# One core, two blocks: attention scores of block 1 and chunk updates of the gated linear attention as fp32r products of stacked parts

## The chip, the cores and the metric

The kernel runs on one core of one Trainium2 chip. The metric is the device time of one execution in microseconds, the median of several runs. Five engines work from queues of their own: TensorE (PE; its weight loads are listed as PEld), VectorE (DVE), ScalarE (ACT), GpSimd (POOL) and SyncE (SP, which here issues the DMAs).

## The reference, cut to what matters

The program computes two transformer blocks in fp32 on 512 tokens of width 1024. The first has 16 meta tokens ahead of the sequence and mixes by sliding-window attention (16 query heads of 64, 4 key heads, sinks) beside a state-space layer; the second has a latent attention and a gated linear attention. The two places that matter:

```python
def block_fn(args):
    n, qn, kn, vn = args
    keys = jnp.concatenate([k_meta, kn], axis=1)
    vals = jnp.concatenate([v_meta, vn], axis=1)
    sc = jnp.einsum('bqkgd,bskd->bkgqs', qn, keys).astype(jnp.float32)
    ...
    p = sink_softmax(sc, mask, sink)
    return jnp.einsum('bkgqs,bskd->bqkgd', p.astype(vals.dtype), vals)
...
    k_dec = k * jnp.exp(tot[:, :, None] - cum).astype(k.dtype)
    upd = jnp.einsum('bnchk,bnchv->nbhkv', k_dec, v).astype(jnp.float32)
    def step(state, inp):
        g, u, qc = inp
        state = state * g[..., None] + u
        return state, jnp.einsum('bchk,bhkv->bchv', qc, state)
```

The first is the attention of 128 queries over 16 meta keys and 256 others; the second the update of the gated linear attention's state by chunks of 64 tokens.

## The kernel before, in words

**Products in three parts.** A fp32 operand is held as two fp32r tiles, a high part and the rest. `fetch` (L144) brings 512 KB of weights into `raw`, ScalarE copies the high part `whi`, VectorE subtracts for `wlo`. A product with weights is three fp32r matmuls: high by high, high by low, low by high (`mm3` L175, `proj` L185, `nat` L190). Products of two activations mostly stay fp32 and show two records each in the trace.

**Order.** The program is written as one sequence; a scheduler orders each engine's queue ahead of time, and the queues do not change at run time. `ps_b`, `ps_q`, `ps_t`, `ps_o` are PSUM banks: in the attention 2, 3, 2 and 1 of them (L679).

**Attention of block 1 (L648 to L804).** Keys: `proj` gives 128 rows, two key heads of 64; each is copied into a tile `kw` of its own whose other 64 rows are zero (L651 to L678), by POOL for one head and ScalarE for the other, in three windows of 16 meta keys and 256 keys. Values are taken by `nat` (L686). `query` (L700) projects 128 rows, two heads of 64 that belong to different key heads, and scales them on VectorE into `q`. There are 8 queries: four ahead and four among the units. A unit is a pair of key heads and 128 tokens, 8 units in all. `scores1` (L716) makes 8 products of 128x272 (128x144 in a first unit of a pair), `q` against `kw` in fp32 (L727), and VectorE adds the mask and takes the maximum (L730). Then the sink, the exponentials on ScalarE and the scaling follow, separately for the two key heads, with ten operations of four columns on VectorE. `turn1` transposes (L759, L769), the results leave PSUM on VectorE for one head and on ScalarE for the other (L771, L773), and `values1` multiplies by the values (L781, L785). The state-space layer (`ssm_quarter`, L569 to L600) is worked in four quarters between the units: its products L569 go through `ps_b`, VectorE takes them out into `sq`, and L591, L592 use what it makes of them.

**Gated linear attention (L1300 to L1420).** `values` (L1344) takes value tokens, 24 matmuls of 256 columns to a group of 128 tokens, and ScalarE copies the group to `gv`; `keys` (L1348) multiplies the decay `ek` by the keys in place on VectorE. `recur` (L1362) forms for each of 4 heads, 4 blocks and 2 chunks the update `ek` x `gv` in fp32 on 64 rows of the array (L1370; the two chunks of a block use the two halves of the rows), VectorE adds it to the state (L1379), and L1381 multiplies by the queries. Value, key, gate and query groups of other heads fill the time between.

Of the kernel before, what the change touches and what calls it, by code (L numbers as in the profile page):

```python
# [9 lines left out]
F32 = mybir.dt.float32  # L10
# [8 lines left out]
P = 128  # L19
D = 1024  # L20
KD = D // P
S = 512
# [31 lines left out]
def body(nc, tc, A, out, es):  # L54
# [593 lines left out]
    with tc.tile_pool(name="m1", bufs=1) as mp:  # L648
        att = mp.tile([P, 8, S], F32, name="att")
        with tc.tile_pool(name="m2", bufs=1) as ap_:  # L650
            kz = [[ap_.tile([P, 3, 272], F32, name=f"kw{mo}{e}") for e in range(2)] for mo in range(2)]  # L651
            for gs in kz:
                for e, g in enumerate(gs):
                    GP.memset(g[64 - 64 * e:128 - 64 * e], 0.0)
# [9 lines left out]
            kw = []  # L664
            for mo in range(2):
                p = proj(wload("w_in", 1024), P, 0, z, C528)
                f = ap_.tile([P, T1], F32, name="kf", tag=f"sq{mo}")
                mul(v2(f), p[:, :, :264], v2(R))

                gs = kz[mo]  # L670
                for e, g in enumerate(gs):
                    r_ = slice(64 * e, 64 * e + 64)
                    cpy = (lambda o, i: act(o, i, AF.Copy)) if e else GP.tensor_copy
                    cpy(g[r_, 0], f[r_, :272])
                    GP.tensor_copy(g[r_, 1:, 0:NM], f[r_, 0:NM].unsqueeze(1).to_broadcast([64, 2, NM]))
                    for n in range(1, 3):
                        cpy(g[r_, n, NM:], f[r_, NM + n * P:NM + (n + 2) * P])
                kw.append(gs)  # L678
# [19 lines left out]
            qf = []  # L698

            def query():  # L700
                p = proj(wload("w_in", 1024), P, 0, z, C512)
                t = (mp if len(qf) < 2 else ap_).tile([P, S], F32, name=f"q{len(qf)}")
                stt(t, p[:, 0, :], 0.125, Rr, ALU.mult, ALU.mult)
                qf.append(t)

            for _ in range(4):
                query()
# [8 lines left out]
            def scores1(u):  # L716
# [861 lines left out]
```

## Time and profile before

| | us |
|---|---|
| median of 3 runs (2582.31 to 2583.71) | 2582.53 |
| the profiled execution's own time | 2580.72 |
| its span | 2578.9 |
| PE busy | 2558.5 (99%) |
| DVE busy | 1577.0 (61%) |
| ACT busy | 993.6 (39%) |
| POOL busy | 84.8 (3%) |

The granted clock of PE was 0.999 of full speed over the span. The span is what the trace covers; the execution's own time lies 1.8 us above it. A matmul's duration is longer than the distance from its start to the next one's, because matmuls overlap in the array; what a matmul costs is therefore read from starts.

### The profile page before, as it was taken

Reading aid. Unit: us, or ns where it says so; the run is one execution under the profiler, and the core shown is the slowest. Engines: PE = TensorE matmul, PEld = TensorE weight load, DVE = VectorE, ACT = ScalarE, POOL = GpSimd, SP = SyncE. Lnnn points to the kernel's source line nnn. Section 1 sums busy time; section 2 is a strip of 40 time slices with the busy share of each in tenths; the row PEclk is TensorE's granted clock in tenths of the full one; section 3 lists DMA queues with packets and bytes.
Section 4 is the critical chain, followed back from the end, with each engine's and each line's share of the span. In section 5 each row is a group of like instructions: output and inputs, shape, how many; then the busy total and the mean of one; then the engine's idle time right before and its main releaser. Section 6 shows DMA issues by size and latency. Waiting matters only on the chain.

```text
span 2578.9 us, 34903 instructions
## 1 busy us (share of the span) xinstructions
PE 2558.5 (99%) x13914; PEld 2181.4 (85%) x13914; DVE 1577.0 (61%) x2866; ACT 993.6 (39%) x1560; POOL 84.8 (3%) x98
## 2 busy tenths in 40 slices
PE   9999999999999999999999999999999999999999
PEld 9999999766888888888888888888878888888887
DVE  7985445685457544468665775555763457655566
ACT  5222223445333222236554454333353234433333
POOL 0000001000000000000000001000000010100000
PEclk9999999999999999999999999999999999999999
DMA  5443324332333333332112223333232222333332
GB/s 183 132 135 110 97 91 135 105 97 63 105 98 96 97 98 98 98 94 70 54 58 62 75 81 108 97 98 98 82 101 66 74 60 83 120 98 98 98 92 73
DMA packets 80774, 243.64 MB, mean 94 GB/s; under 512 B 10418, under 2 KB 20530, under 8 KB 80483
## 3 DMA queue, kind: packets, MB, share of 16 engines
q1 hardware_dynamic: 80610, 241.40, 30.8%
q8 instruction: 110, 1.80, 0.3%
q14 instruction: 54, 0.43, 0.1%
HBM read 229.44 MB, written 11.93 MB: 94 GB/s over the span
## 4 chain that ended last, share of the span: by engine, by line
PE 97%; DVE 2%; ACT 0%; issue 0%; DMA 0%; SPq 0%; DVEq 0%; ACTq 0%
PE ps_b L182 27%; PE ps_q L182 19%; PE ps_t L182 18%; PE mm L182 16%; PE ps_b L198 5%; PE ps_o L1240 1%; PE ps_q L1212 1%; PE ps_q L727 1%; PE ps_o L785 1%; PE ps_t L1228 1%; PE ps_q L1370 1%; DVE sq L66 1%; DVE h L66 0%; PE ps_t L769 0%; PE ps_b L1443 0%; PE ps_q L198 0%
## 5 line engine op out<-in xcount | busy, mean ns | idle before, releaser
L86 ACT ACTIVATE whi<-raw 128x1024 fp32r<-128x1024 f32 (+2 forms) x418 | 432.6, 1038 | 980.9 <-PE ps_b L182 276.3
L66 DVE TENSOR_TENSOR wlo<-raw,whi 128x1024 fp32r<-128x1024 f32 (+2 forms) x418 | 502.4, 1204 | 328.8 <-ACT whi L86 326.6
L182 PE MATMUL ps_b<-zh,whi 128*128 128x512 f32 (+1 forms) x692 | 272.9, 394 | 2.3 <-ACT att L86 0.7
L182 PE MATMUL ps_b<-zl,whi 128*128 128x512 f32 (+1 forms) x692 | 269.7, 390 | 0.0
L182 PE MATMUL ps_b<-zh,wlo 128*128 128x512 f32 (+1 forms) x692 | 269.1, 389 | 0.0
L182 PE MATMUL ps_q<-zh,whi 128*128 128x512 f32 (+1 forms) x488 | 189.3, 388 | 1.2 <-ACT zh L86 1.2
L182 PE MATMUL ps_q<-zl,whi 128*128 128x512 f32 (+1 forms) x488 | 189.4, 388 | 0.0
L182 PE MATMUL ps_q<-zh,wlo 128*128 128x512 f32 (+1 forms) x488 | 189.2, 388 | 0.0
L182 PE MATMUL ps_t<-zh,whi 128*128 128x512 f32 x476 | 185.6, 390 | 0.6 <-ACT zh L86 0.6
L182 PE MATMUL ps_t<-zl,whi 128*128 128x512 f32 x476 | 185.5, 390 | 0.0
L182 PE MATMUL ps_t<-zh,wlo 128*128 128x512 f32 x476 | 185.2, 389 | 0.0
L182 PE MATMUL mm<-zh,whi 128*128 128x264 f32 x800 | 162.5, 284 | 5.7 <-ACT whi L86 5.7
L182 PE MATMUL mm<-zl,whi 128*128 128x264 f32 x800 | 161.8, 284 | 0.0
L182 PE MATMUL mm<-zh,wlo 128*128 128x264 f32 x800 | 161.2, 283 | 0.0
L182 PEld LDWEIGHTS ps_b<-zh,whi 128*128 128x128 f32 (+1 forms) x692 | 129.2, 187 | 33.8 <-issue 2.5
L182 PEld LDWEIGHTS ps_b<-zh,wlo 128*128 128x128 f32 (+1 forms) x692 | 129.2, 187 | 28.6 <-issue 1.1
L182 PEld LDWEIGHTS ps_b<-zl,whi 128*128 128x128 f32 (+1 forms) x692 | 129.3, 187 | 27.2 <-issue 0.7
L182 PEld LDWEIGHTS mm<-zh,whi 128*128 128x128 f32 x800 | 124.3, 189 | 5.8 <-ACT whi L86 5.7
L182 PEld LDWEIGHTS mm<-zl,whi 128*128 128x128 f32 x800 | 124.1, 189 | 0.3 <-DVE zl L83 0.3
L182 PEld LDWEIGHTS mm<-zh,wlo 128*128 128x128 f32 x800 | 124.0, 189 | 0.0
L182 PEld LDWEIGHTS ps_q<-zh,whi 128*128 128x128 f32 x488 | 91.6, 188 | 20.8 <-ACT zh L86 2.0
L182 PEld LDWEIGHTS ps_q<-zl,whi 128*128 128x128 f32 x488 | 91.6, 188 | 20.4 <-DVE zl L66 1.3
(581 smaller groups left out, 5322.2 us busy)
## 6 DMA issues: line engine op xcount, KB each, us to landing
raw<-in_ffn_w_dram SPq DMA_DIRECT2D x130, 512.0 KB, 3.5
raw<-in_w_up_dram SPq DMA_DIRECT2D x88, 512.0 KB, 3.6
raw<-in_w_down_dram SPq DMA_DIRECT2D x44, 512.0 KB, 3.6
raw<-in_w_in_dram SPq DMA_DIRECT2D x32, 512.0 KB, 3.5
raw<-in_mla_o_dram SPq DMA_DIRECT2D x16, 512.0 KB, 3.6
raw<-in_ple_g_dram SPq DMA_DIRECT2D x16, 512.0 KB, 3.7
raw<-in_glu_dram SPq DMA_DIRECT2D x8, 512.0 KB, 3.5
raw<-in_w_out_dram SPq DMA_DIRECT2D x8, 512.0 KB, 3.5
```

Of the source, the lines that this page charges most:

```text
L66: return (e or V).tensor_tensor(o, a, b, op=op)
L86: return SC.activation(o, a, f, **kw)
L182: last["pe"] = PE.matmul(o[:, i, :c1 - c0], lhs, x[k][r][:, c0:c1], start=(k == 0 and j == 0), stop=(k == kt - 1 and j == 2))
L198: PE.matmul(o[:m, :n], x[k][a][:, t0:t0 + m], w[b][:, kk_ * c + m0:kk_ * c + m0 + n], start=(k == 0 and i == 0), stop=(k == kt - 1 and i = ...
L727: last["sc"] = PE.matmul(pq[s_][:, :W], qf[pp * 4 + i][:, n * P:(n + 1) * P], kw[pp][s_][:, max(n - 1, 0), :W])
L785: PE.matmul(po[64 * s_:64 * s_ + 64], vb[n - 1 + j][:, kv * 64:kv * 64 + 64], pT[s_][:, j], start=False, stop=(j == 1))
L1212: PE.matmul(p[:, :N], d["q"][e][:, bs], d["k"][e][:, :N], start=False, stop=True)
L1228: PE.transpose(pt[:, kt * P:(kt + 1) * P], sc[:, kt * P:(kt + 1) * P], ident)
L1240: PE.matmul(po[:, b * P:(b + 1) * P], vt[:, kt, e * P:(e + 1) * P], pT[:, kt * P:(kt + 1) * P], start=(kt == 0), stop=(kt == b))
L1370: PE.matmul(pu[c][:, :256], ek[b][rows, hc], vt[hh][rows, b])
```

## The change

**Attention of block 1.** Both parts of a key head now lie doubled on 128 rows: `kh` holds the high part on both halves, `kl` the rest on both. A unit builds two query tiles `qs`, each of four heads, with the high part in one half of the rows and the rest in the other half. A score is then `qs` x `kh` plus `qs` x `kl`, two fp32r products of 272 columns, or of 256 in a first unit of a pair. `keys(0)` is built ahead of the values, `keys(1)` after the scores of the fourth unit, in the same buffers. The query's scaling is a ScalarE copy; the scale of the norm is applied where the maximum is taken, as a pointer, and the sink is the start of that maximum. The statistics of two heads share a tile of eight columns, with four small operations on VectorE and one small exponential to a unit. All transposed results leave PSUM on ScalarE. Four weight tiles are fetched ahead of the keys.

**Gated linear attention.** The key tile is split into `kd`, high part and rest stacked on 128 rows, one per chunk; the values become `gvh` (high part on both halves, four ScalarE copies to a group) and `gvl` (the rest on the own half, zero on the other, two VectorE subtractions). An update is two fp32r products on all 128 rows.

```diff
-        att = mp.tile([P, 8, S], F32, name="att")
+        att = [mp.tile([P, 4, S], F32, name="att0")]
         with tc.tile_pool(name="m2", bufs=1) as ap_:
-            kz = [[ap_.tile([P, 3, 272], F32, name=f"kw{mo}{e}") for e in range(2)] for mo in range(2)]
-            for gs in kz:
-                for e, g in enumerate(gs):
-                    GP.memset(g[64 - 64 * e:128 - 64 * e], 0.0)
...
+            for _ in range(4):
+                fetch("w_in", 1024)
+            kf = []
             for mo in range(2):
                 p = proj(wload("w_in", 1024), P, 0, z, C528)
-                f = ap_.tile([P, T1], F32, name="kf", tag=f"sq{mo}")
+                f = zp.tile([P, aw], F32, name="acc") if mo else ap_.tile([P, T1], F32, name="kf", tag="sq0")
                 mul(v2(f), p[:, :, :264], v2(R))
-
-                gs = kz[mo]
-                for e, g in enumerate(gs):
-                    r_ = slice(64 * e, 64 * e + 64)
-                    cpy = (lambda o, i: act(o, i, AF.Copy)) if e else GP.tensor_copy
-                    cpy(g[r_, 0], f[r_, :272])
-                    GP.tensor_copy(g[r_, 1:, 0:NM], f[r_, 0:NM].unsqueeze(1).to_broadcast([64, 2, NM]))
-                    for n in range(1, 3):
-                        cpy(g[r_, n, NM:], f[r_, NM + n * P:NM + (n + 2) * P])
-                kw.append(gs)
+                kf.append(f)
+
+            def keys(pp):
+
+                out_ = []
+                for e in range(2):
+                    a = slice(64 * e, 64 * e + 64)
+                    f = kf[pp][a]
+                    kh, kl = (ap_.tile([P, 3, 272], F32R, name=f"k{n}{e}") for n in "hl")
+                    for o in (a, slice(64 - 64 * e, 128 - 64 * e)):
+                        for w_, c in ((0, f[:, :272]), *((n, f[:, NM + n * P:NM + (n + 2) * P]) for n in (1, 2))):
+                            t = slice(NM if w_ else 0, 272)
+                            act(kh[o, w_, t], c, AF.Copy)
+                            sub(kl[o, w_, t], c, kh[a, w_, t].bitcast(F32))
+                        for k in (kh, kl):
+                            GP.tensor_copy(k[o, 1:, :NM], k[o, 0:1, :NM].to_broadcast([64, 2, NM]))
+                    out_.append((kh, kl))
+                return out_
+
+            kw = {0: keys(0)}
...
-            qf = []
-
-            def query():
+            qf = [mp.tile([P, 4, S], F32, name=f"q{i}") for i in range(2)]
+
+            def query(i):
                 p = proj(wload("w_in", 1024), P, 0, z, C512)
-                t = (mp if len(qf) < 2 else ap_).tile([P, S], F32, name=f"q{len(qf)}")
-                stt(t, p[:, 0, :], 0.125, Rr, ALU.mult, ALU.mult)
-                qf.append(t)
-
-            for _ in range(4):
-                query()
+                act(qf[i // 4][:, i % 4], p[:, 0], AF.Copy, scale=0.125)
+
+            for i in range(4):
+                query(i)
...
-                st = [[sm.tile([P, 4], F32, name=f"at{j}{s_}", bufs=2) for j in range(3)] for s_ in range(2)]
+                mx, dn, nb = (sm.tile([P, 8], F32, name=f"at{j}", bufs=2) for j in range(3))
+                sk = sink[:, pp * 8:pp * 8 + 8]
+
+                qs = []
+                for s_ in range(2):
+                    t = ap_.tile([P, 4, P], F32R, name=f"qs{s_}", bufs=2)
+                    a, o = slice(64 * s_, 64 * s_ + 64), slice(64 - 64 * s_, 128 - 64 * s_)
+                    x = qf[pp][a, :, n * P:(n + 1) * P]
+                    act(t[a], x, AF.Copy)
+                    sub(t[o], x, t[a].bitcast(F32))
+                    qs.append(t)
                 for i in range(4):
                     pq = [pss("q"), pss("q")]
                     for s_ in range(2):
-                        last["sc"] = PE.matmul(pq[s_][:, :W], qf[pp * 4 + i][:, n * P:(n + 1) * P],
-                                               kw[pp][s_][:, max(n - 1, 0), :W])
+                        for k in range(2):
+                            last["sc"] = PE.matmul(pq[s_][:, :max(W, 256)], qs[s_][:, i],
+                                                   kw[pp][s_][k][:, max(n - 1, 0), :max(W, 256)],
+                                                   start=(k == 0), stop=(k == 1))
                     for s_ in range(2):
-                        V.tensor_tensor_reduce(sc[s_][:, i, :W], pq[s_][:, :W], mk, 1.0, -3.0e38,
-                                               ALU.add, ALU.max, st[s_][0][:, i:i + 1])
+                        c = s_ * 4 + i
+                        V.tensor_tensor_reduce(sc[s_][:, i, :W], pq[s_][:, :W], mk, r[:, n:n + 1], sk[:, c:c + 1],
+                                               ALU.add, ALU.max, mx[:, c:c + 1])
+                ts(nb, mx, -1.0)
+                sub(mx, sk, mx)
+                act(mx, mx, AF.Exp)
                 for s_ in range(2):
-                    mx, dn, nb = st[s_]
...
-                    tt(mx, mx, sk, ALU.max)
-                    ts(nb, mx, -1.0)
-                    sub(mx, sk, mx)
-                    act(mx, mx, AF.Exp)
...
-                    add(dn, dn, mx)
-                    V.reciprocal(dn, dn)
...
+                add(dn, dn, mx)
+                V.reciprocal(dn, dn)
...
                 live[u] = sc, mt
...
-                        if s_:
-                            V.tensor_copy(pT[:, j], pt)
-                        else:
-                            act(pT[:, j], pt, AF.Copy)
+                        act(pT[:, j], pt, AF.Copy)
...
-                act(att[:, pp * 4:pp * 4 + 4, n * P:(n + 1) * P], po.rearrange("p (i q) -> p i q", i=4), AF.Copy)
+                act(att[pp][:, :, n * P:(n + 1) * P], po.rearrange("p (i q) -> p i q", i=4), AF.Copy)
...
-                    query()
+                    query(4 + ui)
+                if ui == 3:
+                    kw[1] = keys(1)
+                if ui == 4:
+                    att.append(mp.tile([P, 4, S], F32, name="att1", tag="q0"))
                 elif 5 <= ui < 8:
                     gate(zp.tile([P, aw], F32, name="acc" if ui == 5 else "sq", bufs=1 if ui == 5 else 2)[:, :S])
                 elif ui == 8:
+                    gt = mp.tile([P, 4, S], F32, name="gt", tag="q1")
                     with tc.issue_after(last["sc"].ins):
                         for i in range(2):
-                            gate(mp.tile([P, S], F32, name=f"q{i}"))
+                            gate(gt[:, i])
...
+        kd = [[mp.tile([P, S], F32R, name=f"kd{b}{c}", bufs=1) for c in range(2)] for b in range(4)]
+        ch = lambda c: slice(64 * c, 64 * c + 64)
+        vl = [mp.tile([P, 2, 256], F32R, name=f"gvl{i}", bufs=1) for i in range(6)]
+        for t in vl:
+            for c in range(2):
+                ts(t[ch(1 - c), c], mask[ch(1 - c), :256], 0.0)
...
-            t = qt[i] = mp.tile([P, 4, 2, P], F32, name=f"gq{i}", bufs=1)
+            t = qt[i] = mp.tile([P, 4, 2, P], F32, name="gq")
...
         def values(i):
-            t = vt[i] = mp.tile([P, 4, 256], F32, name=f"gv{i}", bufs=1)
-            return token("gla_v", lambda b, p: act(t[:, b], p, AF.Copy))
-
-        def keys(c):
-            return token("gla_k", lambda b, p: mul(ek[b][:, c * 256:(c + 1) * 256], ek[b][:, c * 256:(c + 1) * 256], p))
+
+            t = vt[i] = []
+
+            def evac(b, p):
+                h_, l = mp.tile([P, 2, 256], F32R, name="gvh", bufs=6), vl[(4 * i + b) % 6]
+                t.append((h_, l))
+                for c in range(2):
+                    act(h_[ch(c), c], p[ch(c)], AF.Copy)
+                    act(h_[ch(1 - c), c], p[ch(c)], AF.Copy)
+                    sub(l[ch(c), c], p[ch(c)], h_[ch(c), c].bitcast(F32))
+
+            return token("gla_v", evac)
+
+        def keys(i):
+            cols = slice(i * 256, i * 256 + 256)
+
+            def evac(b, p):
+                t = ek[b][:, cols]
+                mul(t, t, p)
+                for c in range(2):
+                    k = kd[b][c][:, cols]
+                    act(k[ch(c)], t[ch(c)], AF.Copy)
+                    sub(k[ch(1 - c)], t[ch(c)], k[ch(c)].bitcast(F32))
+
+            return token("gla_k", evac)
...
-                    rows = slice(64 * c, 64 * c + 64)
-                    PE.matmul(pu[c][:, :256], ek[b][rows, hc], vt[hh][rows, b])
+                    for i, t in enumerate(vt[hh][b]):
+                        PE.matmul(pu[c][:, :256], kd[b][c][:, hc], t[:, c], start=(i == 0), stop=(i == 1))
...
-            o = ob[hh] = mp.tile([P, 4, 256], F32, name="ob", bufs=4)
+            o = ob[hh] = mp.tile([P, 4, 256], F32, name="ob")
```

On PE, at the first scores of the attention, before (`q` and `kw` are queries and keys, `U` the state-space input, `zh` and `zl` the normed activations; numbers tell tiles apart):

```order
L182 MATMUL ps_b<-zh_4679,wlo 128x512
L727 MATMUL ps_q<-kw_4749,q_5315 128x144
L727 MATMUL ps_q<-kw_4750,q_5315 128x144
L727 MATMUL ps_q<-kw_4749,q_5348 128x144
L569 MATMUL ps_b<-U,bstl 128x132 x4
L727 MATMUL ps_q<-kw_4750,q_5348 128x144
L727 MATMUL ps_q<-kw_4749,q_5381 128x144
L727 MATMUL ps_q<-kw_4750,q_5381 128x144
L569 MATMUL ps_b<-U,bstl 128x132 x4
L727 MATMUL ps_q<-kw_4749,q_5414 128x144
L727 MATMUL ps_q<-kw_4750,q_5414 128x144
```

And now, with `kh`, `kl` the doubled keys and `qs` the stacked queries:

```order
L182 MATMUL ps_b<-zh_4679,wlo 128x512
L569 MATMUL ps_b<-U,bstl 128x132 x6
L744 MATMUL ps_q<-kh_5117,qs_5433 128x256
L744 MATMUL ps_q<-kl_5118,qs_5433 128x256
L569 MATMUL ps_b<-U,bstl 128x132 x2
L590 MATMUL ps_b<-U,M 128x128
L744 MATMUL ps_q<-kh_5135,qs_5436 128x256
L744 MATMUL ps_q<-kl_5136,qs_5436 128x256
L744 MATMUL ps_q<-kh_5117,qs_5433 128x256
L744 MATMUL ps_q<-kl_5118,qs_5433 128x256
L744 MATMUL ps_q<-kh_5135,qs_5436 128x256
L744 MATMUL ps_q<-kl_5136,qs_5436 128x256
```

Six of the eight first state-space products now stand ahead of the first score, and a score waits for a `qs` rather than for a `q`.

On DVE, at the same place, before (ISA rows are the masked maxima):

```order
L83 SCALAR_TENSOR_TENSOR q_5414<-ps_b,R 128x512
L730 ISA sc,at_5420<-ps_q,mask 128x144
L730 ISA at_5420 128x1
L730 ISA sc,at_5423<-ps_q,mask 128x144
L730 ISA at_5423 128x1
L730 ISA sc,at_5420<-ps_q,mask 128x144
L730 ISA at_5420 128x1
L66 TENSOR_TENSOR wlo<-raw,whi 128x1024
L66 TENSOR_TENSOR sq_5491<-ps_b,tab 128x264
L66 TENSOR_TENSOR sq_5494<-ps_b,tab 128x264
L66 TENSOR_TENSOR sq_5492<-ps_b,tab 128x264
L66 TENSOR_TENSOR sq_5493<-ps_b,tab 128x264
```

And now:

```order
L66 TENSOR_TENSOR sq_5505<-ps_b,tab 128x264
L66 TENSOR_TENSOR sq_5508<-ps_b,tab 128x264
L66 TENSOR_TENSOR wlo<-raw,whi 128x1024
L66 TENSOR_TENSOR sq_5506<-ps_b,tab 128x264
L66 TENSOR_TENSOR qs_5433<-q_5296,qs_5433 64x512
L66 TENSOR_TENSOR sq_5507<-ps_b,tab 128x264
L66 TENSOR_TENSOR sq_5505<-ps_b,tab 128x264
L66 TENSOR_TENSOR sq_5508<-ps_b,tab 128x264
L66 TENSOR_TENSOR qs_5436<-q_5296,qs_5436 64x512
L66 TENSOR_TENSOR qs_5602<-q_5296,qs_5602 64x512
L66 TENSOR_TENSOR qs_5605<-q_5296,qs_5605 64x512
L749 ISA sc,at_5430<-ps_q,mask,sink,rs_y 128x144
```

Four subtractions of `qs`, for the first two units, stand between the state-space evacuations, the first of the maxima comes behind them, and the scaling of a query is gone.

On ACT, in the gated linear attention where the third head's values are taken, before:

```order
L86 ACTIVATE R<-ps_s 128x512
L86 ACTIVATE whi<-raw 128x1024 x2
L86 ACTIVATE zh_17792<-ps_t 128x512
L86 ACTIVATE gv_17108<-ps_b 128x256 x3
L86 ACTIVATE whi<-raw 128x1024 x2
L86 ACTIVATE gv_17108<-ps_b 128x256
```

And now:

```order
L86 ACTIVATE whi<-raw 128x1024 x2
L86 ACTIVATE kd_16862<-ek_16854 64x256
L86 ACTIVATE kd_16863<-ek_16854 64x256
L86 ACTIVATE gvh<-ps_b 64x256 x10
L86 ACTIVATE zh_18017<-ps_q 128x512
L86 ACTIVATE S<-ps_q 128x256
L86 ACTIVATE gvh<-ps_b 64x256 x2
L86 ACTIVATE whi<-raw 128x1024 x2
```

A group of values takes four copies of 64 rows where it took one of 128, and copies for the split of the keys stand ahead of them.

## Rows read from the trace of the kernel before

**Rows 1.** The page: busy time of the engines, and the chain that ended last by engine.

```profile
PE 2558.5 (99%) x13914; PEld 2181.4 (85%) x13914; DVE 1577.0 (61%) x2866; ACT 993.6 (39%) x1560; POOL 84.8 (3%) x98
...
PE 97%; DVE 2%; ACT 0%; issue 0%; DMA 0%; SPq 0%; DVEq 0%; ACTq 0%
```

**Rows 2.** Windows: busy time of each engine (instructions) in stretches named by microsecond.

```profile
core 0: us, PE busy (x) PEld busy (x) DVE busy (x) ACT busy (x) POOL busy (x), PEclk, DMA share, GB/s
100.00:200.00 100.00, 100.00 (x832) 99.29 (x832) 87.64 (x163) 27.82 (x34) 0.00 (x0) 1.00 0.48 147
...
477.00:492.00 15.00, 12.81 (x70) 10.57 (x68) 14.12 (x44) 5.94 (x21) 0.00 (x0) 1.00 0.28 83
...
1925.00:1963.00 38.00, 38.00 (x246) 31.79 (x245) 12.42 (x14) 23.03 (x33) 0.00 (x0) 1.00 0.24 69
1963.00:2097.00 134.00, 134.00 (x917) 117.21 (x916) 64.12 (x145) 37.66 (x69) 9.60 (x13) 1.00 0.24 72
```

**Rows 3.** Waits of PE in 474 to 626 us: total, times, longest.

```profile
PE ps_b L591 <- DVE sq L66: 2.0, 2, 1.3
PE ps_b L569 <- DVE sq L66: 1.0, 1, 1.0
```

**Rows 4.** Timeline of PE around scores: start, duration, instruction; two records make one fp32 product.

```profile
496.39 1.54 PE L727 MATMUL ps_q<-kw,q 128*128 128x272 f32 x6
497.77 0.60 PE L759 MATMUL ps_t<-ident,mt 128*64 128x128 f32 x4
```

**Rows 5.** Timeline of PE, 535.97 us on: two-record score of 144 columns, and what follows.

```profile
535.97 0.41 PE L727 MATMUL ps_q<-kw,q 128*128 128x144 f32 x2
536.21 0.60 PE L769 MATMUL ps_t<-ident,sc 128*128 128x128 f32 x4
```

**Rows 6.** Timeline of PE in the gated linear attention: chunk updates L1370 between fp32r products.

```profile
1963.39 0.28 PE L198 MATMUL ps_q<-wlo,zh 128*128 128x256 f32 x1
1963.60 0.70 PE L1370 MATMUL ps_q<-gv,ek 64*128 64x256 f32 x2
1964.23 0.39 PE L198 MATMUL ps_b<-whi,zh 128*128 128x256 f32 x1
1964.45 0.28 PE L198 MATMUL ps_b<-whi,zl 128*128 128x256 f32 x1
...
1980.08 0.70 PE L1370 MATMUL ps_q<-gv,ek 64*128 64x256 f32 x4
1980.71 0.39 PE L198 MATMUL ps_b<-whi,zh 128*128 128x256 f32 x1
```

**Rows 7.** Groups of 1963 to 2097 us: evacuations of values and keys.

```profile
L86 ACT ACTIVATE gv<-ps_b 128x256 f32<-128x256 f32 x12 | 4.5, 379 | 31.5 <-PE ps_b L198 31.5
L66 DVE TENSOR_TENSOR ek<-ek,ps_b 128x256 f32<-128x256 f32 x4 | 1.6, 412 | 0.8 <-PE ps_b L198 0.8
```

**Rows 8.** Groups of 477 to 626 us: ScalarE and VectorE beside the scores.

```profile
L86 ACT ACTIVATE sc<-sc,at 128x272 f32<-128x272 f32 x48 | 24.4, 509 | 6.3 <-DVE at L79 6.3
L730 DVE CUSTOM_DVE_ANT_0 sc<-ps_q,mask 128x272 f32<-128x272 f32 x48 | 20.4, 436 | 10.9 <-PE ps_q L727 10.7
L771 DVE COPY pT<-ps_t 128x512 f32<-128x512 f32 x12 | 8.2, 686 | 1.7 <-PE ps_t L769 1.7
L86 ACT ACTIVATE pT<-ps_t 128x512 f32<-128x512 f32 x14 | 8.1, 583 | 0.8 <-PE ps_t L769 0.7
L66 DVE TENSOR_TENSOR at<-at,sink 128x4 f32<-128x4 f32 x16 | 2.3, 158 | 0.1
```

**Rows 9.** Groups of 1300 to 1960 us (other attention): splits of 64x512, masked maximum with pointer scale.

```profile
L66 DVE TENSOR_TENSOR qr<-qr,qr 64x512 fp32r<-64x512 f32 x8 | 5.5, 686 | 0.5 <-ACT qr L86 0.3
L86 ACT ACTIVATE qr<-qr 64x512 fp32r<-64x512 f32 x8 | 5.0, 629 | 2.4 <-DVE qr L66 2.3
L1215 DVE CUSTOM_DVE_ANT_0 sc<-ps_q,mmask,ovr 128x256 f32<-128x256 f32 x9 | 4.3, 483 | 0.9 <-PE ps_q L1212 0.3
```

**Rows 10.** Groups of 440 to 478 us: key copies on ScalarE.

```profile
L86 ACT ACTIVATE kw<-kf 64x256 f32<-64x256 f32 x2 | 0.7, 398 | 0.0
```

More of the change, by code (lines that the diff above doesn't have):

```diff
@@ L729, in scores1 @@
                     for s_ in range(2):
-                        V.tensor_tensor_reduce(sc[s_][:, i, :W], pq[s_][:, :W], mk, 1.0, -3.0e38,
-                                               ALU.add, ALU.max, st[s_][0][:, i:i + 1])
-                for s_ in range(2):
-                    mx, dn, nb = st[s_]
-                    t = sc[s_]
-                    kv = 2 * pp + s_
-                    sk = sink[:, kv * 4:kv * 4 + 4]
-                    tt(mx, mx, sk, ALU.max)
-                    ts(nb, mx, -1.0)
-                    sub(mx, sk, mx)
-                    act(mx, mx, AF.Exp)
-                    for i in range(4):
-                        act(t[:, i, :W], t[:, i, :W], AF.Exp, bias=nb[:, i:i + 1], accum_out=dn[:, i:i + 1])
-                    add(dn, dn, mx)
-                    V.reciprocal(dn, dn)
-                    mul(mt[:, :, 32 * s_:32 * s_ + NM], t[:, :, :NM], dn.unsqueeze(2).to_broadcast([P, 4, NM]))
+                        c = s_ * 4 + i
@@ new lines, in scores1 @@
+                        V.tensor_tensor_reduce(sc[s_][:, i, :W], pq[s_][:, :W], mk, r[:, n:n + 1], sk[:, c:c + 1],
[3 more added lines that the diff above has]
+                act(mx, mx, AF.Exp)
+                for s_ in range(2):
+                    for i in range(4):
+                        c = s_ * 4 + i
+                        act(sc[s_][:, i, :W], sc[s_][:, i, :W], AF.Exp, bias=nb[:, c:c + 1], accum_out=dn[:, c:c + 1])
@@ L746, in scores1 @@
+                add(dn, dn, mx)
+                V.reciprocal(dn, dn)
+                for s_ in range(2):
+                    t, d = sc[s_], dn[:, s_ * 4:s_ * 4 + 4]
+                    mul(mt[:, :, 32 * s_:32 * s_ + NM], t[:, :, :NM], d.unsqueeze(2).to_broadcast([P, 4, NM]))
                     if s_:
                         for i in range(4):
-                            act(t[:, i, NM:W], t[:, i, NM:W], AF.Copy, scale=dn[:, i:i + 1])
+                            act(t[:, i, NM:W], t[:, i, NM:W], AF.Copy, scale=d[:, i:i + 1])
@@ L749, in scores1 @@
                     else:
-                        mul(t[:, :, NM:W], t[:, :, NM:W], dn.unsqueeze(2).to_broadcast([P, 4, W - NM]))
+                        mul(t[:, :, NM:W], t[:, :, NM:W], d.unsqueeze(2).to_broadcast([P, 4, W - NM]))
                 live[u] = sc, mt
@@ L825, in body @@
                 ga, gs = gate_tiles[2 * i:2 * i + 2]
-                stt(ga, ga, 1.0, att[:, i], ALU.add, ALU.mult)
+                stt(ga, ga, 1.0, att[i // 4][:, i % 4], ALU.add, ALU.mult)
                 wg = wload("glu", 1024)
```

1 line of the change is left out of this document (removed).

## The prediction, made before the changed kernel was run

> **What bounds the kernel now.** I read the page first: PE is busy 99% of the span, and the chain of work that ended last lies 97% on PE, 2% on DVE [rows 1]. So a microsecond of PE work counts in full unless PE then waits instead. Next the windows around the two places [rows 2]. In the gated linear attention, 1963 to 2097 us, PE is busy 134.00 of 134.00, while DVE has 64.12 and ACT 37.66: there is cover for work beside PE. The attention of block 1 is different at its start: from 477 to 492 us DVE is busy 14.12 of 15.00 and PE only 12.81, so DVE sets the pace there. The table of PE's waits says the same: 2.0 and 1.0 us in front of the state-space products, both for `sq`, which DVE evacuates [rows 3]. The granted clock is 1.00 in every window, the upper level, so no term below depends on it.
>
> **The price of a product.** The reader is to take distances between starts. A fp32 score of 272 columns: six records, three products, start at 496.39 and the next instruction at 497.77, 1.38/3 = 0.46 us [rows 4]. One of 144 columns: 536.21 - 535.97 = 0.24 us [rows 5]. For fp32r, the window of 100 to 200 us is filled by 832 matmuls of 264 columns: 100/832 = 0.120 us [rows 2].
>
> **Scores.** Before: 48 x 0.46 + 16 x 0.24 = 25.9 us. After: 64 scores of two products are 128; at 0.120 us, and 0.121 for the 272 columns, 15.5 us. Gain 10.4 us. In the changed order some ten groups of scores come to stand next to work on part of the array; the border beside a 64-row product costs about 0.10 us (the next part works it out) [rows 6], so I take off 1.0 us.
>
> **Chunk updates.** The kernel has 32 of them, in 26 groups: 20 with one product (x2 records) and 6 with both chunks (x4). The last fp32r product before one starts at 1963.39, the update at 1963.60, the next fp32r products at 1964.23 and 1964.45 [rows 6]. Where neighbours stand 0.12 us apart, this is 0.21 before, 0.63 itself and 0.22 after: 0.63 + 0.09 + 0.10 = 0.82 us a group. The x4 group from 1980.08 to 1980.71 takes the same 0.63. So 26 x 0.82 = 21.3 us. After: 64 fp32r products of 256 columns on the whole array, at 0.12 us, are 7.7 us. Gain 13.6 us.
>
> The rows show that two products on the two row halves share one 0.63. The Trainium skill, "TensorEngine Tiling (Array Packing)", section Key Properties, says that different tiles work in parallel, which speaks against giving the row halves up: if all pairs ran so, the work before would be 16 x 0.82 = 13.1 us and the gain 5.4. The trace agrees for 6 pairs and shows the other 20 updates alone, each at the full price; the sum goes by those groups.
>
> **Evacuations in the gated linear attention.** A copy of 64x256 on ACT takes 0.398 [rows 10], a VectorE operation on 128x256 from PSUM 0.412 [rows 7]. ACT gets 64 + 16 copies for 16 of 0.379: +25.8 us; DVE 32 + 16 subtractions: +19.8, and 12 fills, at most 0.4 each, some 4. From 1925 to 2097 us ACT was busy 60.7 of 172 and DVE 76.5 [rows 2]; both stay under 60%. That hides the sums but not the holding of a bank: a group of values leaves its bank after 4 x 0.398 + 2 x 0.412 = 2.4 us at most instead of 0.38, with two `ps_b` banks and 24 x 0.12 = 2.9 us of PE work to a group. The margin is 0.5 us, and copies of weights or normalised rows can stand ahead in the queue. None of it waits: 0. All 16 groups wait half a microsecond beyond: 8 us. I take 2 us, since the early groups have six banks to turn through.
>
> **Start of the attention.** In the DVE-bound stretch DVE gets the `qs` subtractions of units 0 to 3, eight of 0.686 [rows 9] = 5.5 us, and loses two query scalings of the size of L771, 0.686 [rows 8], and some short statistics, 0.5 in all: net +3.6 us. PE waits there for `sq`, so these come out as waiting: 3.6 us. Behind them on DVE stand `sq` evacuations and the maxima; PE waits for both. The chain to a first score also gets longer, by a ScalarE split of 0.629 [rows 9].
>
> **The rest of the attention.** DVE there: -9.6 (14 transposed results of 0.686 [rows 8]), -4.1 (six more scalings), +5.5 (`qs` of units 4 to 7), +5.0 (12 splits for `keys(1)` at 0.412 [rows 7]); the maximum with a pointer took 0.483 on 256 columns, the one with constants 0.436 on 272 [rows 8, 9], so 64 x 0.06 = +4, or up to 8 if the second pointer costs as much. The sum is about nothing: DVE isn't relieved, though fewer short operations remain. ACT gets 14 x 0.583, 8 x 0.6, 16 x 0.629 and 12 x 0.40: +28 us. `keys(1)` is one block of 12 x 0.4 = 4.8 us in ACT's queue, ahead of exponentials and transposed results for which PE waits with two `ps_t` banks. Bounds 0 and, for a block at each engine of the pair, 10; I take 2.5, half the block, because PE still has projections to do. `keys(0)` has the same 4.8 us, ahead of the values; four query projections of 24 products follow, so 1 us, bounds 0 and 4.8. GpSimd's eight small copies per `keys` are needed only by the later units: 0. The DMA queue carries the same transfers in nearly the same order: 0.
>
> **Sum.** 10.4 - 1.0 + 13.6 = 23.0 us of PE work gone; waits 2 + 3.6 + 2.5 + 1 = 9.1 come. Net 13.9 us against the profiled execution's 2580.72: 2566.8. The median of the runs stands 1.8 above that execution, so **2568.6 us** as a median. A measurement of this kernel can tell about 0.2%, or 5.2 us, from no change.
>
> **Rivals.**
> (1) *The cover holds*, chance 0.18: none of the new waits comes; all that is gained on PE shows, 2582.5 - 23.0 = 2559.5. For it: PE was never idle in the second place [rows 2]. Against: the start of the attention.
> (2) *VectorE and ScalarE eat the first gain*, chance 0.18: their chains to a score and from it set the attention's length, which stays as it was or grows by 5 us; left are 13.6 - 2 = 11.6 or 6.6 us: 2571 to 2576, up to 2580 if the value banks wait at all groups too. For it: 14.12 of 15 us of DVE [rows 2].
> (3) *The updates bring little*, chance 0.07: two row halves work side by side more often than I counted, and the gain there is 5.4 instead of 13.6: 2568.6 + 8.2 = 2576.8. Beside it stands the page named above. Against it: the 20 single groups. That fp32r scores aren't cheaper at all is excluded by 0.120 against 0.46.
> (4) *Slower*, chance 0.07: ScalarE becomes the bound of the attention. A unit has five PSUM results of 0.583 and eight exponentials of 0.509 [rows 8] on it, 2.9 + 4.1 us, now with splits and key copies. If the exponentials of one unit stand ahead of the results of the other, PE holds at two full `ps_t` banks once per unit. To end 5.2 us above before, waits must grow by 13.9 + 5.2 = 19.1, 2.4 us at each of 8 units; a whole block of 4.1 us each time gives 33 us, 2601. Against it: in the stage before, what PE waits for longest is DVE, not ACT [rows 3].
>
> **How the numbers follow.** The forecast has 0.50, its own range 2564 to 2574. The range 2559 to 2579 takes in most of it, of (1) and of (2), and (3). Faster by over 0.2% (under 2577.4): 0.49 + 0.18 + 0.11 + 0.04 = 0.82; within 0.2%: 0.11; slower: 0.07.
>
> **What would show it.** In the profile after: two scores of 272 columns standing 0.12 us apart; updates as 64 instructions of one record each, 0.12 apart, no 0.21 before them; the window of the updates' stage shorter by 10 to 14 us with PE still at 100%. PE's waits in the attention should name `qs` or `sq` at the start, some 6 us in all, and `pT` or a score's tile around the fifth unit. The forecast is wrong if PE's waits in the attention pass 15 us, or if waits for `gvh` or `gvl` show more than 5.

## The result: slower by 0.6%, and the profile after

| | before | changed |
|---|---|---|
| median, us | 2583.12 (4 runs) | 2600.23 (4 runs) |
| ratio, 95% interval | | 1.0063 (1.0051 to 1.0076) |
| span of the profiled execution, us | 2578.9 | 2600.1 |

The forecast of 2568.6 us and its range, 2559 to 2579, missed on the wrong side: 17 us slower, where 14 were to be gained. The page of the changed kernel, busy times and the chain:

```profile
PE 2563.0 (99%) x13914; PEld 2182.8 (84%) x13914; DVE 1609.2 (62%) x2896; ACT 1045.7 (40%) x1672; POOL 84.8 (3%) x100
...
PE 95%; DVE 3%; ACT 1%; issue 0%; DMA 0%; SPq 0%; DVEq 0%; ACTq 0%
```

Against [rows 1], PE is busy 4.5 us longer, although the change took work from it, and 2 points of the chain moved to DVE and ACT. Where is the loss? First the attention, from its first state-space product to its last value product. Windows of before, then of the changed kernel (columns as in [rows 2]: length, then PE, PEld, DVE, ACT and POOL busy, the granted clock, DMA share, GB/s):

```profile
478.42:629.26 150.84, 145.89 (x715) 101.73 (x714) 116.61 (x353) 78.23 (x229) 3.78 (x10) 1.00 0.29 88
```

```profile
479.57:640.29 160.72, 145.94 (x721) 102.55 (x719) 124.58 (x314) 102.25 (x268) 6.43 (x18) 0.96 0.27 83
```

The stage is 9.9 us longer. PE's idle time in it went from 150.84 - 145.89 = 5.0 us to 14.8, DVE's work rose by 8.0, and the granted clock is no longer 1.00. PE's waits from 440 to 660 us, where [rows 3] had 2.0 and 1.0:

```profile
PE ps_t L776 <- DVE mt L66: 2.8, 2, 2.5
PE ps_q L744 <- DVE at L749: 2.6, 4, 0.9
PE ps_b L198 <- DVE acc L66: 2.5, 1, 2.5
PE ps_b L569 <- DVE at L66: 1.6, 1, 1.6
PE ps_b L590 <- issue: 1.3, 1, 1.3
PE ps_b L592 <- DVE sq L66: 1.2, 1, 1.2
PE ps_q L744 <- DVE qs L66: 1.0, 1, 1.0
```

Five of the seven lines are waits within the stage for a result of DVE: normalised scores (`mt`), maxima (`at`), splits (`qs`), the state-space layer (`sq`). The wait for `acc`, the second key tile, comes ahead of the stage.

Then a loss where nothing was changed. From the last value product of the attention to the first product of the gated linear attention (629.3 to 1928.4 us before, 640.3 to 1952.5 now) the program is the same but for 19 products of 256 columns that now stand ahead of the gated linear attention instead of in it, about 2 us of work; yet it takes 13 us more. The chain shows why, in products of 24 matmuls of 512 columns; before:

```profile
696.12 5.44 PE ps_q L182 x24
701.56 5.44 PE ps_t L182 x24
```

and after:

```profile
691.29 5.49 PE ps_b L182 x24
696.78 5.49 PE ps_q L182 x24
```

That is 0.2267 and 0.2288 us a matmul, at a granted clock of 1.00 in both. This is the sort of difference that a table of waits cannot show: PE is busy all the time, only slower.

In the gated linear attention 19 of the 32 updates look as forecast, two records, 0.12 us apart. Nine others stand right behind a state product in fp32, and there the second record comes 0.30 us after the first. One of the 19, with nothing lost at its borders (compare [rows 6]):

```profile
1990.93 0.28 PE L198 MATMUL ps_q<-whi,zh 128*128 128x256 f32 x1
...
1991.83 0.28 PE L198 MATMUL ps_q<-wlo,zh 128*128 128x256 f32 x1
1991.95 0.28 PE L1416 MATMUL ps_q<-gvh,kd 128*128 128x256 f32 x1
1992.07 0.28 PE L1416 MATMUL ps_q<-gvl,kd 128*128 128x256 f32 x1
1992.19 0.29 PE L198 MATMUL ps_b<-whi,zh 128*128 128x256 f32 x1
```

### The profile page after: what moved, and what is told of

The parts are those of the page before. It is cut to its first block, busy times and chain, and to the rows that moved or that the text cites. A ratio compares the mean times of both kernels' runs of the same rounds, so it can differ in the third digit from the quotient of the medians.

```text
span 2600.1 us, 35098 instructions
## 1 busy us (share of the span) xinstructions
PE 2563.0 (99%) x13914; PEld 2182.8 (84%) x13914; DVE 1609.2 (62%) x2896; ACT 1045.7 (40%) x1672; POOL 84.8 (3%) x100
## 4 chain that ended last, share of the span: by engine, by line
PE 95%; DVE 3%; ACT 1%; issue 0%; DMA 0%; SPq 0%; DVEq 0%; ACTq 0%
PE ps_b L182 27%; PE ps_q L182 19%; PE ps_t L182 19%; PE mm L182 16%; PE ps_b L198 5%; PE ps_o L1259 1%; PE ps_q L1231 1%; PE ps_o L799 1%; PE ps_t L1247 1%; DVE sq L66 1%; PE ps_t L786 0%; PE ps_b L1489 0%; PE ps_q L744 0%; PE ps_q L1229 0%; PE ps_q L1230 0%
```

## The experiments

### Addresses

The statistics of two heads in one tile made six tiles of 32 bytes out of twelve. Their pool lies under that of the normed activations, so every activation tile moved down by 6 x 32 = 192 bytes, while the weight buffers, which lie under both, stayed. The first two runs undo this in the changed kernel (e1), and do it alone in the kernel before (e2).

```diff
             live = {}
+            sm.tile([P, 48], F32, name="pad", bufs=1)
```

> The changed kernel with one unused tile of 192 bytes in the pool of small statistics, so that every normed activation, the moving operand of the three-part products, lies at the SBUF address it had before; the instructions are the same. Theory A (address): since the statistics tiles went from 12 to 6, all activations lie 192 bytes lower, and that alone lengthens each fp32r product of 512 columns from 0.2267 to 0.2289 us; 7470 of them are 15 us. It expects 2585 us (2582 to 2588) and a spacing of 0.2267. Theory B (a slower pace brought about by the waits in the attention, the clock, or the longer program): no effect, 2600 us (2598 to 2602) and 0.2289.

Measured: 2592.0 us (2590.3 to 2594.4), 8.2 less than the changed kernel; 24 matmuls take 5.44 us again.

```profile
692.82 5.44 PE ps_b L182 x24
698.26 5.44 PE ps_q L182 x24
```

```diff
-    zp.tile([P, 64], F32, name="gap")
+    zp.tile([P, 16], F32, name="gap")
...
-    zp.tile([P, 80], F32, name="gap")
+    zp.tile([P, 32], F32, name="gap")
```

> The kernel before with its two spacer tiles made 192 bytes smaller, so that the activations lie where the changed kernel has them; nothing else differs. Theory A (address): slower by 15 us, 2598 us (2595 to 2601), spacing 0.2289 for 512 columns. Theory B: 2583 us as before, spacing 0.2267.

Measured: 2594.2 us, ratio 1.0041 (1.0026 to 1.0056): 10.0 us slower than before, by spacers alone.

```profile
697.23 5.49 PE ps_q L182 x24
702.73 5.49 PE ps_t L182 x24
```

On PE, e2 runs the same instructions in the same order as the kernel before. The spacing is that of theory A in both runs, and B falls; the times miss A's ranges, by 4 us in e1 and 1 us in e2. The 15 us were too many, in part because the same shift makes products of 256 columns faster: in the changed kernel nine of them fit between 1990.93 and about 1991.95, 0.113 us each, where 0.12 was the distance before. Means over the products with weights in the whole traces are 0.1152 and 0.1195 us, some 1100 products, 5 us back.

Five more runs, g1 to g5, ask for the rule. The first two change the spacers of the kernel before by +32 and -96 bytes; the third and fourth those of e8 (below) by -32 and -64; the fifth moves the weight buffers up by 192 bytes, with most other tiles that lie under the activations, and keeps every activation in place.

> The kernel before with its spacers 32 bytes larger, so that the first column of each 512-column product lies on a multiple of 256 bytes; before it lay 32 bytes under one, in the changed kernel 32 bytes over one. If only the place of before is fast: spacing 0.229 us and 2593 us. If lying at or under a multiple is what counts: 0.2267 and 2583.

> The kernel before with its spacers 96 bytes smaller: the first column of each 512-column product lies half way between multiples of 256 bytes. If only the place of before is fast: 0.229 us and 2593 us. If it is the place just over a multiple that is slow: 0.2267 and 2583. The products of 256 columns, which take the activations as their fixed operand, were faster with the shift of the change (0.115 against 0.119 us); here anything from 0.115 to 0.120.

> e8 (the gated linear attention part with copies split) with its spacers 32 bytes smaller: products of 512 columns start 64 bytes under a multiple of 256 instead of 32 under. Measured so far: 32 under 0.2270 us, 32 over 0.2291, on it 0.2333, half way 0.2342. If nearness to the old place counts: 0.227 to 0.229, 2574 to 2590. A gain is possible only down to the 0.226 that the fastest single products show, 7 us.

> The same with 64 bytes smaller spacers, 96 under a multiple. As above: 0.227 to 0.234 us, 2574 to 2630.

> The kernel before with the weight buffers (raw, high and low parts) 192 bytes higher and every activation where it was. The distance between the two operands of a product is then what it is in the changed kernel, while the address of the activations is that of before. If the activations' own address decides: 0.2267 us for 512 columns, 2583 us. If the distance between weights and activations decides: 0.2291 and 2593.

Measured: 2625.2 (one run), 2640.9 (one run), 2617.5 (4 runs; e8 itself has 2574.8), 2625.8 (one run) and 2597.1 us (one run, 2585.9 before in the same job). A line of the chain of each, in this order:

```profile
699.45 5.60 PE ps_q L182 x24
```

```profile
694.85 5.62 PE ps_q L182 x24
```

```profile
699.40 5.60 PE ps_q L182 x24
```

```profile
690.76 5.60 PE ps_b L182 x24
```

```profile
696.34 5.49 PE ps_q L183 x24
```

The fifth run decides: the activations are where they were before, only the weights moved, and the pace is that of the changed kernel. So the address of the activations alone doesn't decide; the distance between the two operands of a product accounts for every run here. That moving both together leaves the pace as it was is not shown, no run tried it. Take the distance of the kernel before as 0 and count modulo 256 bytes: 0 gives 5.44, 64 gives 5.49 (three kernels), 32, 192 and 224 give 5.60, 160 gives 5.62. Nearness is worth nothing, and no distance was found that beats 0. That 256 is the modulus, and why the distance matters, isn't shown.

### One half of the change at a time

e3 is the kernel before with the gated linear attention of the changed one; e4 has the attention of the changed one and the tile of e1.

> Only the second part of the change: the chunk updates of the gated linear attention as stacked fp32r products, the attention and all addresses ahead of it as before. Both theories: faster by 8 to 12 us, 2571 to 2575 us; the forecast's price list gives 2571.5 (13.6 gained, 2 lost to waits). If the updates bring nothing, 2583.

> Only the first part of the change, with the unused tile of 192 bytes, so at the addresses of before; the updates of the gated linear attention as before. The forecast gave this part a gain of 2 us. By the traces its stage is longer by about 10 us: theory A expects 2590 to 2594 us, with PE waiting for VectorE at the start and the granted clock at its lower level for some stretches of the stage. Theory B expects the slower pace here too, 2605 us or more.

Measured: e3 2580.0 us, ratio 0.9986 (0.9976 to 0.9995), 4.3 us faster; e4 2596.3 us, ratio 1.0047 (1.0030 to 1.0063), 12.1 us slower, in both cases against 2584.2 of the same job. Both are slower than forecast, e3 by 5 us and e4 by 2 against theory A. With 8.2 for the addresses, 12.1 - 4.3 + 8.2 = 16.0 of the 17.1 us are placed.

### Gated linear attention: where half the gain went

Windows of before and of e3, first the stretch from the gate products to the first state product, then from there to the last:

```profile
1928.40:1968.40 40.00, 40.00 (x256) 33.08 (x255) 12.66 (x15) 22.26 (x30) 0.00 (x0) 1.00 0.28 81
...
1968.40:2101.00 132.60, 132.60 (x908) 116.35 (x908) 62.24 (x144) 36.00 (x66) 10.34 (x14) 1.00 0.23 67
```

```profile
1932.50:1976.10 43.60, 41.74 (x239) 35.28 (x239) 18.98 (x31) 30.07 (x50) 0.00 (x0) 0.88 0.23 70
...
1976.10:2099.50 123.40, 121.07 (x909) 115.72 (x907) 75.21 (x176) 52.72 (x110) 12.16 (x18) 1.00 0.23 73
```

The second stretch is 9.2 us shorter. The first is 3.6 longer, though 17 products of 256 columns have left it: PE waits 1.9 us there for the decay, which ScalarE makes and which now stands behind the copies of the first head's values, and the granted clock is 0.88. At the lower of the clock's two levels, half of the upper one, work takes twice as long; a mean of 0.88 over 43.6 us stands for up to 43.6 x 0.12 = 5 us lost, more than the wait.

```profile
PE ps_s L1316 <- ACT ek L86: 1.9, 1, 1.9
```

e8 gives eight of these copies to VectorE:

```diff
-                    act(h_[ch(1 - c), c], p[ch(c)], AF.Copy)
+                    if i:
+                        act(h_[ch(1 - c), c], p[ch(c)], AF.Copy)
+                    else:
+                        V.tensor_copy(h_[ch(1 - c), c], p[ch(c)])
```

> Only the gated linear attention part (e3), with the second copies of the first head's values on VectorE instead of ScalarE: 8 copies of 0.38 us leave ScalarE in the stretch ahead of the updates, where PE waited 1.9 us for the decay that ScalarE makes, and where the stretch was 3.6 us longer than before. If ScalarE's queue is what cost that, the stretch shortens by 2 to 3.5 us: 2576.5 to 2578. If the lower granted clock there comes whatever the queue, 2580 as e3.

Measured: 2574.8 us (2573.7 to 2577.2), ratio 0.9965 (0.9953 to 0.9976): 9.0 us faster than before and the fastest kernel of this study. Its runs and those of e3 do not overlap. The stretch shrinks by 4.0 us, more than the copies' own time. The wait for the decay gives 0.8 of them, it is still 1.1 us; the clock in the stretch rises too, and the up to 5 us lost to it become up to 1.6:

```profile
1932.70:1972.30 39.60, 38.54 (x239) 32.27 (x239) 22.49 (x39) 27.49 (x42) 0.00 (x0) 0.96 0.25 78
```

```profile
PE ps_s L1316 <- ACT ek L86: 1.1, 1, 1.1
```

The lower clock there does not come from the copies alone. e4, which leaves this part as it was, shows 0.92 in the stretch, with PE busy throughout, and takes 43.0 us for what took 40.0 before:

```profile
1943.60:1986.60 43.00, 43.00 (x256) 36.15 (x255) 12.67 (x15) 22.28 (x30) 0.00 (x0) 0.92 0.24 76
```

So why the clock fell in this stretch stays open, and some 3 us of the loss in this execution of e4 lie where nothing was changed.

### Attention: what makes it longer

e5, e6 and e7 take the attention part (e4) and change the load of VectorE by -7.7, -11.0 and +9.6 us.

```diff
-                        V.tensor_tensor_reduce(sc[s_][:, i, :W], pq[s_][:, :W], mk, r[:, n:n + 1], sk[:, c:c + 1],
+                        V.tensor_tensor_reduce(sc[s_][:, i, :W], pq[s_][:, :W], mk, 1.0, -3.0e38,
```

> The attention part alone at the old addresses (e4), but the masked maximum takes constants (scale 1, start -3e38) instead of the two pointers. It leaves out the scale of the norm in the queries and the sink in the maximum. In e4 the maximum took 0.556 us on 272 columns and 0.423 on 144, with constants it took 0.436 and 0.300 before: 64 x 0.12 = 7.7 us of VectorE work go. Theory C (VectorE sets the length of the attention): the stage shortens by 5 to 8 us, 2588 to 2591 us. Theory D (ScalarE, or the longer chain from query to score, sets it): within 2 us of e4's 2596.

```diff
-                    sub(t[o], x, t[a].bitcast(F32))
+                    sub(t[o], x, t[a].bitcast(F32), GP)
```

> e4 with the 16 subtractions of the stacked queries on GpSimd instead of VectorE: 11.0 us of VectorE work go, at the price of a slower operation ahead of each unit's scores (a GpSimd product of 128x256 took 0.738 us, so some 1.5 us for 64x512 against 0.686). Theory C: faster than e4 by 6 to 10 us, 2586 to 2590. Theory D (the chain to a score): 2596 to 2600, since the chain gets longer by 0.8 us per unit.

```diff
-                        act(pT[:, j], pt, AF.Copy)
+                        if s_:
+                            V.tensor_copy(pT[:, j], pt)
+                        else:
+                            act(pT[:, j], pt, AF.Copy)
```

> e4 with the 14 transposed results of one head back on VectorE as before: VectorE gets 9.6 us more, ScalarE 8.1 us less. Theory C: slower than e4, 2600 to 2605. Theory D with ScalarE as the bound: faster by 3 to 8, 2588 to 2593.

Measured: e5 2596.0, e6 2598.4, e7 2600.7 us, against 2596.3 for e4. Less work on VectorE gave nothing; more of it cost 4.4 (the runs of e7 and e4 do not overlap, their 95% intervals do). By the numbers on record e5 and e6 speak for D, e7 for C. f1 and f2 then part the attention otherwise: f1 keeps only the new products, f2 only the statistics and the moves to ScalarE.

```diff
-                        last["sc"] = PE.matmul(pq[s_][:, :W], qf[pp * 4 + i][:, n * P:(n + 1) * P],
-                                               kw[pp][s_][:, max(n - 1, 0), :W])
+                        for k in range(2):
+                            last["sc"] = PE.matmul(pq[s_][:, :max(W, 256)], qs[s_][:, i],
+                                                   kw[pp][s_][k][:, max(n - 1, 0), :max(W, 256)],
+                                                   start=(k == 0), stop=(k == 1))
```

> The attention part with only its products changed: doubled keys, stacked queries, two fp32r products; the scaling of the queries, the maxima, the statistics and the transposed results stay as before. PE work falls as in e4, VectorE gets 11.0 us of query splits and 5.1 of key splits on top and loses nothing. Theory E (the shorter scores only leave PE waiting, because the splits lengthen the way from query to score on engines that set the pace, and the lower clock follows the waits): 2596 to 2603 us. Theory F (the moves to ScalarE and the pointer forms do the damage): 2576 to 2585.

```diff
-                        V.tensor_tensor_reduce(sc[s_][:, i, :W], pq[s_][:, :W], mk, 1.0, -3.0e38,
-                                               ALU.add, ALU.max, st[s_][0][:, i:i + 1])
+                        V.tensor_tensor_reduce(sc[s_][:, i, :W], pq[s_][:, :W], mk, r[:, n:n + 1], sk[:, c:c + 1],
+                                               ALU.add, ALU.max, mx[:, c:c + 1])
```

> The other half of the attention part: fp32 scores with padded keys as before, but query scaling and all transposed results on ScalarE, pointer maxima, statistics of two heads in one tile; addresses as before. VectorE loses 9.6 + 5.5 us of copies and some 6 of short operations and gets 7.7 for the pointers. Theory E: 2578 to 2584 us, no loss or a small gain. Theory F: 2588 to 2597, most of e4's 12 us.

Measured: f1 2608.4 us, ratio 1.0092 (1.0075 to 1.0109), 24 us slower, beyond even what E gave; f2 2587.4, ratio 1.0013 (1.0003 to 1.0022), 3.4 slower, between the theories. So the products, with the splits that they need, do the damage, and the statistics win back 12 us of it, though alone they are no gain either. The windows of the stage in e4, e5, f1 and f2, in this order:

```profile
480.59:641.16 160.57, 144.78 (x720) 101.22 (x719) 124.54 (x314) 102.30 (x268) 6.44 (x18) 0.97 0.27 83
```

```profile
481.43:641.61 160.18, 147.41 (x720) 104.46 (x719) 117.06 (x314) 102.61 (x268) 6.75 (x18) 0.94 0.28 83
```

```profile
480.83:652.11 171.28, 153.36 (x720) 107.54 (x719) 133.21 (x381) 93.91 (x257) 6.51 (x18) 0.90 0.26 78
```

```profile
479.10:631.26 152.16, 145.70 (x714) 99.72 (x712) 108.32 (x284) 88.39 (x240) 3.76 (x10) 1.00 0.28 87
```

Read the clock beside the idle time. Each window is of one execution (e4 2598.9 us, f1 2610.0), so a few us between two of them say little. A stage of 160 us at a mean clock of 0.97 has lost up to 5 us to the lower level; at 0.94 it is 10, in f1 at 0.90 it is 17. In e5 PE idles 12.8 us instead of 15.8, as theory C wants, but the clock took up to 5 us more, and nothing was left of it. In f1 PE did little from 505 to 515 us, and then had work at half speed, 1.2 of 2.4 GHz:

```profile
500.00:505.00 5.00, 3.90 (x28) 3.38 (x28) 4.85 (x20) 2.13 (x6) 0.52 (x1) 1.00 0.57 194
505.00:510.00 5.00, 2.58 (x14) 1.92 (x12) 2.80 (x14) 4.13 (x17) 0.00 (x0) 0.84 0.68 219
510.00:515.00 5.00, 2.53 (x10) 1.91 (x10) 3.26 (x15) 3.37 (x13) 0.31 (x1) 0.50 0.02 3
515.00:520.00 5.00, 4.46 (x16) 3.56 (x16) 4.21 (x15) 3.62 (x13) 0.00 (x0) 0.50 0.23 52
520.00:525.00 5.00, 5.00 (x12) 2.11 (x10) 2.80 (x13) 1.71 (x4) 0.00 (x0) 0.50 0.00 0
```

The Trainium skill, "TensorE: Matmul & The Clock Gate", section "What's actually happening", says that recent activity of TensorE sets its clock; these rows agree, while the 0.92 of e4 above, with PE busy throughout, is not explained by a table of busy time. Whether the clock is the cause of the longer stage, two runs with filler work ask:

```diff
-                        for k in range(2):
+                        for k in (0, 1, 0, 1):
```

> The attention part alone at the old addresses (e4), with each pair of score products issued twice into the same bank, the second pair starting afresh: PE work of a score goes back to 0.48 us, about what the fp32 product took, and nothing else changes. Theory G (the shorter scores leave TensorE waiting on VectorE, and its granted clock then falls to the lower level for stretches in which there is work): with the filler the clock stays up, the stage costs no more than in e4 although it has 15 us more PE work: 2588 to 2596 us. Theory H (the waits alone, the clock being a bystander): the filler partly goes into waits, the rest adds: 2598 to 2606.

> The same filler in the products-only kernel (f1), whose attention had 34 us at the lower clock, up to 17 us lost by it. Theory G: 2592 to 2602 us, faster than f1 by 6 or more with 15 us more PE work. Theory H: 2608 to 2618.

Measured: e9 2600.3 us, as H has it, 4.0 more than e4; f1b 2605.4 us (2602.7 to 2605.7), ratio 1.0082 (1.0066 to 1.0099), between G and H, 3.0 less than f1 with 15 us more to do. The intervals of f1 and f1b overlap, so a gain isn't shown; that the 15 us did not come on top is. The windows, e9 and f1b:

```profile
481.26:647.43 166.17, 156.39 (x848) 116.01 (x847) 124.57 (x314) 101.98 (x268) 6.23 (x18) 0.98 0.26 80
```

```profile
481.96:649.69 167.73, 157.09 (x849) 115.31 (x847) 133.92 (x381) 93.58 (x257) 7.61 (x18) 0.98 0.26 80
```

In f1b PE's idle time fell from 17.9 to 10.6 us, and the clock went up from 0.90 to 0.98, worth up to 14 us of the stage; together they paid for the filler. The idle time alone would have left some 8 us on top, so in f1 the lower clock was a part of the loss. In e9 it rose only from 0.97 to 0.98; of 15 us of filler 6 went into PE's idle time (15.8 to 9.8), and the stage grew by 5.6. So in the changed kernel the waits come first and the lower clock adds to them. How much of the waiting is VectorE's load, how much ScalarE's and how much the longer way from query to score stays open, because e5 to e7, and the two runs with filler, also got another order from the scheduler. VectorE itself waits for ScalarE's exponentials in the changed kernel, 5.1 us ahead of one kind of sum where it was 1.3 before (before, then changed):

```profile
L66 DVE TENSOR_TENSOR at<-at,at 128x4 f32<-128x4 f32 x16 | 2.4, 157 | 2.6 <-ACT sc L86 1.3 <-ACT at L86 1.1
```

```profile
L66 DVE TENSOR_TENSOR at<-at,at 128x8 f32<-128x8 f32 x8 | 1.3, 157 | 5.7 <-ACT sc L86 5.1 <-ACT at L86 0.6
```

## Why the prediction was wrong

**The addresses** were in no term. The diff shows the cause, twelve tiles of a pool made six, and the spacers in the code say that somebody had placed things; I read both and drew nothing from it. Measured: 8.2 us in the changed kernel, 10.0 in the kernel before.

**Scores.** The price of 0.12 us a product held for about a third of them. In e4, 61 of the 64 scores ran at the full clock; the second product came up to 0.13 us behind the first in 23 of these, and 0.19 to 0.245 us behind it in 37. For example, with no idle time shown between:

```profile
502.84 0.39 PE L745 MATMUL ps_q<-kh,qs 128*128 128x272 f32 x1
503.07 0.29 PE L745 MATMUL ps_q<-kl,qs 128*128 128x272 f32 x1
503.32 0.39 PE L745 MATMUL ps_q<-kh,qs 128*128 128x272 f32 x1
503.55 0.29 PE L745 MATMUL ps_q<-kl,qs 128*128 128x272 f32 x1
```

So the 9.4 us did not all appear: PE's busy time fell by 145.89 - 144.78 = 1.1 us, with up to 4.8 us of lower clock in it, so about 6 us of work went; 37 x 0.09 = 3.3 us is about the rest. Eleven of the 64 scores start within 0.06 us of the end of a masked maximum on VectorE, four before, so some of them now go at the pace of VectorE's maxima. Why the other second products come late isn't shown.

**The start and the rest of the attention** is the step that failed: "VectorE: the sum is about nothing", and 3.6 + 2.5 us of waits. Measured in e4: VectorE's busy time +7.9 us, idle PE +10.8, clock up to 4.8. Forecast for the whole attention was a gain of 2.3 us, measured a loss of 12.1. PE's idle time in the changed kernel's stage, 14.8 us, even stayed under the 15 that I gave as a sign of being wrong. One term missed in the sum on VectorE is the maximum with two pointers, where I took +4 and allowed 8:

```profile
L749 DVE CUSTOM_DVE_ANT_0 sc<-ps_q,mask,sink 128x272 f32<-128x272 f32 x48 | 25.6, 555 | 15.2 <-PE ps_q L744 8.7 <-PE ps_t L786 6.4
L749 DVE CUSTOM_DVE_ANT_0 sc<-ps_q,mask,sink 128x144 f32<-128x144 f32 x16 | 6.2, 422 | 1.1 <-PE ps_q L744 1.1
```

It takes 0.555 us where [rows 8] has 0.436: 0.12 a time, 7.7 us. The upper bound was the right end; the 0.483 of [rows 9] was for one pointer. The `qs` splits cost 0.686 as [rows 9] said. The wait of the keys ahead of the values was 2.5 us, where I took 1.

**"The granted clock is 1.00 in every window, so no term depends on it"** was wrong as a conclusion: with the new waits the clock of the attention came to 0.96, and in e4 it was 0.92 even in a stretch without waits. This step should have had a bound: a stretch at the lower level costs half of its length in PE work.

**Updates of the gated linear attention.** The count of 26 groups was right, and the 9.2 us of the second stretch are more than the 5.4 that rival (3) left. The price was somewhat high: of the 26 groups before, 10 stand between fp32r products on both sides, as the one that I priced; the others have a state product or a transpose at one side. After, 19 of 32 pairs stand 0.12 us apart. So PE's busy time in the stretch fell by 132.60 - 121.07 = 11.5 us. Of the 13.6 less 2 us forecast, 4.3 came: 9.2 in the stretch itself, with 2.3 us of new idle time of PE in it, less the longer stretch ahead of it. The wait forecast was for value banks; the one that came was for the decay behind value copies in ScalarE's queue, 1.9 us, with a lower clock that no term had, up to 5 us. e8 cut the wait to 1.1 and the clock's share to 1.6.

**The rivals.** Rival (2) had the mechanism of the attention, DVE at 14.12 of 15 us, but stopped at a loss of 5 us. Rival (4), the one on the slow side, named ScalarE and full `ps_t` banks; the one wait of PE of this kind in the changed kernel, for `pTm`, was 0.5 us. So the sign was on record with 0.07, on a mechanism that did not come.

```profile
PE ps_t L786 <- ACT pTm L86: 0.5, 1, 0.5
```

## What to carry to other kernels

Where one engine waits for another at the start of a stage, shorter work on the first buys waits, and the waits may buy a lower clock for the work behind them: price both before counting the gain. Look at what a change does to the sizes of pools: every tile above a pool that shrinks moves, and here 192 bytes less between the two operands of a matmul cost 0.9% of each one of 512 columns. To separate such an effect from the change, pad the pool back to its size, one line, and run both.

## What the runs showed that was not expected

- The pace of an fp32r product of 512 columns goes with the distance between its operands in a partition: 5.44 to 5.62 us for 24, up to 57 us in this kernel (2640.9 against 2584.0). The products of 264 columns hardly moved for most of these distances.
- The same shift makes 512 columns slower and 256 faster (0.2267 to 0.2288, 0.1195 to 0.1152 us), so no single distance tried serves both.
- A masked maximum costs 0.12 us more when both of its scalars are pointers, on 272 and on 144 columns alike (0.555 against 0.436 us, 0.422 against 0.300): a price per instruction.
- Filler work of 15 us on PE did not lengthen one kernel (f1 2608.4, f1b 2605.4 us): it went into idle time and came with a mean clock of 0.98 instead of 0.90 in the stage.
